# Four plain head jobs instead of eight, with the block sums formed in place

## The chip, the core and the metric

The kernel runs on one core of a Trainium2 chip, in one launch. The metric is device time in microseconds, median over runs; lower is better. The core has five engines with a queue each, which run side by side and wait for one another through semaphores: TensorE (PE, products, with its weight loads PEld), VectorE (DVE), ScalarE (ACT), GpSimd (POOL) and SyncE (SP, which here issues most DMAs).

## What is computed

One step of a hybrid decoder layer, in float32, for a prompt of 1024 tokens and for 8 samples of 4 tokens each. Cut to what matters:

```python
def layer(x, c, C0, n0, m0, k_past, v_past, ...):
    h, gate = adaln_in(x, c, w_ada, b_ada, g_norm)          # RMS norm, scale and shift from c
    (mq, mk, mv, mi, mf, mo, mz, aq, ak, av, az, gm, ga) = split_in(h @ w_in)
    y_m, C, n, m = mlstm_branch(mq, mk, mv, mi, mf, mo, mz, C0, n0, m0, ...)   # 4 heads, chunks of 128
    q, k = partial_rope(aq, pos), partial_rope(ak, pos)
    o = attn_prompt(q, k, v, sinks)                          # window of 128, 8 heads, 2 kv heads
    y_a = o * silu(az)
    u = sigmoid(gm) * (y_m @ w_mo) + sigmoid(ga) * (y_a @ w_ao)
    return x + gate * (u @ w_o), C, n, m, k_keep, v_keep     # then a final RMS norm
```

`h @ w_in` is the largest part. Its columns are cut into matrices of 128 columns: for each of the 4 mLSTM heads `mq`, `mk`, `mv`, `mo` and `mz`; `ak`, `av`, four `aq` and four `az` for the attention; eight `ga` and eight `gm` for the gates.

## The kernel before

**Exact products from two halves.** Each float32 operand is split into a high part and a low part of a faster format (`hi`, `lo`): ScalarE casts the high part, VectorE subtracts it for the low part. A product is then three matmuls: hi x hi, hi x lo, lo x hi.

**Plain jobs.** `job(n, ...)` multiplies the 128 columns of one matrix with all 1056 tokens: three pieces of 384, 384 and 288 columns (`PIECES`), in each 8 blocks of the depth with three matmuls, so 72 matmuls a job. While a job runs, the next one's weights are split (`prefetch`) and those of the one after are loaded (`preload`). `order` lists the plain jobs: `ak`, `av`, four `aq`, eight of the twelve head matrices, and later eight `w_mo`. The list `inner` has the head matrices in the order mq, mk, mv of head 0, then of head 1, and so on.

**Pairs of block products.** The other matrices go two by two through `block_products`: the 2 x 2 blocks of (depth half, token half) and the two matrices are multiplied in 7 block products in place of 8 (Winograd's form), each of 4 blocks of the depth with three matmuls of 512 columns. The products need sums of blocks of h: `t1` to `t4`, each with a high and a low part in half tiles. `sum_blocks` forms `t3`, `t2` and `t4` first, block by block of the depth (`k`), then `t1`, which takes the place of one block of h itself and must therefore wait until the last plain job is done. The samples' 32 columns go by themselves: 16 small products per pair (`Pair.samples`, tile `smp`) and one that gathers them (`samples_end`, tile `smpo`). Pairs in order: two of head matrices, eight `gate`, two `query_gate`, four `head_gate`.

**Half tiles.** `ht` hands out tiles of 128 x 512 from one pool of 43; x itself (16 tiles, `xT`), the sums, the attention's tiles and the heads' all come from it. After the setup x (by then h, scaled and shifted) is stored to `hD` in DRAM, and `sum_blocks` loads its blocks again from there.

**What fills the gaps.** The order of the instructions on each engine is written while the program is built. `Side` keeps a running clock `now`, an estimate that each matmul moves on, and a few streams of generators: "m" (gates, then the heads' recurrences `head(h)`, two at a time, 35 apart), "a" (the transposes of k and v, then 16 attention units `unit(g, b0)`, at most five at a time), "x" (`sum_blocks`, and `att_sums` at the end), "s" (the samples' attention, then the samples' heads `sample_head`), "g" (`ada_gate`, then `out_weights`). Between the matmuls of a job `side.tick()` takes a due generator one step on. Each `yield` names the time until the next step and the kind of PSUM bank that this needs. `side.finish` and `side.until` run a stream on where its result is needed. Loads and stores that SP issues stand in SP's one queue in the order in which they were written; most stores are put off by 8.0 (`store`).

**Where things stand.** `ada_gate` and `sample_attention` are added after the four query jobs; `sum_blocks` when the fourth job from the end of the plain ones begins (`i == -4`); the samples' heads when the last head is done (`h == NH-1`); the output weights at product 6 of pair 4 (`OUT_WEIGHTS`). With the last plain job (`i == -1`) the scores of the attention move from the bank kind "a" to "o", and the first pair is loaded.

## Time and profile before

| what | value |
|---|---|
| median of 3 runs | 844.07 us (842.58 to 844.69) |
| the profiled execution | 845.38 us, its span 843.6 us |
| PE busy | 823.8 us, 98% |
| DVE busy | 607.4 us, 72% |
| ACT busy | 417.2 us, 49% |
| POOL busy | 62.9 us, 7% |
| mean granted TensorE clock | 0.995 of full speed |
| DMA moved | 158.18 MB, mean 188 GB/s |

The span is the time between the first and the last instruction of the profiled execution; 1.8 us lie around it. Times of one instruction are given as the profile has them; successive instructions of an engine overlap a little, so a run of equal instructions, divided by their number, gives the price of one. Names such as `g_mk` or `bx` are the tiles that an instruction writes: `g_<matrix>` the result of a plain job, `bx`, `by`, `bw` and `bz` those of the block products, `sc`, `pt` and `oT` the attention's, `S`, `U`, `n` and `C` the heads'.

### The profile page before, as it was taken

The page shows a single profiled execution, that of the slowest core. Times are in us where ns is not written, and L with a number is a line of the kernel's source. Part 1 is how long each engine was busy: PE and PEld are TensorE (multiplying, and loading weights), DVE is VectorE, ACT ScalarE, POOL GpSimd, SP SyncE. Part 2 cuts the span into 40 slices and gives each one's busy share as a digit, 9 for nine tenths or more (in the row PEclk, how much of TensorE's full clock was granted, in tenths as well). Part 3 has the DMA queues.
Part 4 walks back from the last instruction along what each step waited for, and adds up shares of the span by engine and source line. Part 5 has one row for each costly group of instructions (what it writes and reads, how often), then busy time and mean ns, then how long its engine had stood idle before and what let it go on. Part 6 is the DMA issues. An engine that isn't in the chain of part 4 may idle for free.

```text
span 843.6 us, 15348 instructions
## 1 busy us (share of the span) xinstructions
PE 823.8 (98%) x5181; PEld 681.4 (81%) x5181; DVE 607.4 (72%) x1607; ACT 417.2 (49%) x1025; POOL 62.9 (7%) x108
## 2 busy tenths in 40 slices
PE   6999999999999999999999999999999999999996
PEld 2679989888899888888787777777777779997775
DVE  4786884655875775756676776788878998974676
ACT  4763356655664654545453534444436554334343
POOL 0120000001000000000000000000002104250000
PEclk9999999999999999999999999999999999999998
DMA  9996549257746553356456484555446676634522
GB/s 320 378 357 200 147 148 301 99 172 257 223 122 207 165 172 121 133 165 210 164 197 215 146 252 127 177 152 151 127 126 204 199 264 202 219 131 137 200 106 107
DMA packets 117859, 158.18 MB, mean 188 GB/s; under 512 B 29056, under 2 KB 64512, under 8 KB 117748
## 3 DMA queue, kind: packets, MB, share of 16 engines
q1 hardware_dynamic: 111556, 146.44, 54.1%
q10 hardware_dynamic: 4752, 6.56, 2.2%
q0 software_dynamic: 1472, 4.20, 1.3%
q8 instruction: 41, 0.67, 0.3%
q14 instruction: 38, 0.31, 0.1%
HBM read 113.41 MB, written 44.75 MB: 187 GB/s over the span
## 4 chain that ended last, share of the span: by engine, by line
PE 91%; DMA 4%; DVE 3%; ACT 1%; issue 1%; SPq 0%; DVEq 0%; ACTq 0%
PE by L258 10%; PE bx L258 10%; PE bw L258 9%; PE g_aq L258 6%; PE g_w_mo L258 6%; PE bz L258 5%; PE g_mq L258 4%; PE g_mk L258 4%; PE g_mv L258 3%; PE foW L258 3%; PE foX L258 3%; PE foY L258 2%; PE sc L258 2%; PE oT L258 2%; PE foZ L258 2%; PE smp L258 2%
## 5 line engine op out<-in xcount | busy, mean ns | idle before, releaser
L219 ACT ACTIVATE p<-p,nmx 128x256 f32<-128x256 f32 (+1 forms) x64 | 31.0, 486 | 23.9 <-DVE nmx L219 19.7
L258 PE MATMUL g_aq<-h_h,wh_aq 128*128 128x384 f32 (+1 forms) x96 | 32.4, 337 | 0.0
L219 DVE CUSTOM_DVE_ANT_0 p<-sc,cst,sink 128x256 f32<-128x256 f32 (+1 forms) x64 | 26.1, 463 | 7.4 <-PE sc L258 5.4
L258 PE MATMUL g_w_mo<-ym_l,wh_w_mo 128*128 128x384 f32 (+1 forms) x96 | 31.1, 324 | 0.0
L258 PE MATMUL g_aq<-h_l,wh_aq 128*128 128x384 f32 (+1 forms) x96 | 31.0, 323 | 0.0
L258 PE MATMUL g_w_mo<-ym_l,wl_w_mo 128*128 128x384 f32 (+1 forms) x96 | 31.0, 323 | 0.0
L258 PE MATMUL g_aq<-h_h,wl_aq 128*128 128x384 f32 (+1 forms) x96 | 31.0, 323 | 0.0
L258 PE MATMUL g_w_mo<-ym_h,wh_w_mo 128*128 128x384 f32 (+1 forms) x96 | 31.0, 323 | 0.0
L258 PE MATMUL g_mq<-h_h,wh_mq 128*128 128x384 f32 (+1 forms) x72 | 24.7, 343 | 0.0
L258 PE MATMUL g_mk<-h_h,wh_mk 128*128 128x384 f32 (+1 forms) x72 | 24.6, 342 | 0.0
L258 PE MATMUL g_mq<-h_l,wh_mq 128*128 128x384 f32 (+1 forms) x72 | 23.3, 323 | 0.0
L258 PE MATMUL g_mk<-h_h,wl_mk 128*128 128x384 f32 (+1 forms) x72 | 23.3, 323 | 0.0
L258 PE MATMUL g_mk<-h_l,wh_mk 128*128 128x384 f32 (+1 forms) x72 | 23.3, 323 | 0.0
L258 PE MATMUL g_mq<-h_h,wl_mq 128*128 128x384 f32 (+1 forms) x72 | 23.2, 322 | 0.0
L246 POOL DMA_DIRECT2D oD<-uqv x16 | 8.8, 551 | 147.1 <-ACT uqv L219 147.1
L258 PEld LDWEIGHTS g_aq<-h_h,wh_aq 128*128 128x128 f32 x96 | 18.0, 188 | 1.4 <-issue 1.2
L219 ACT ACTIVATE gt<-gt 128x512 f32<-128x512 f32 (+1 forms) x17 | 10.4, 612 | 16.9 <-DVE gt L219 16.2
L258 PEld LDWEIGHTS g_aq<-h_l,wh_aq 128*128 128x128 f32 x96 | 18.1, 188 | 0.0
L258 PEld LDWEIGHTS g_w_mo<-ym_l,wh_w_mo 128*128 128x128 f32 x96 | 18.0, 188 | 0.0
L258 PEld LDWEIGHTS g_w_mo<-ym_h,wh_w_mo 128*128 128x128 f32 x96 | 18.0, 188 | 0.0
L258 PEld LDWEIGHTS g_aq<-h_h,wl_aq 128*128 128x128 f32 x96 | 18.0, 188 | 0.0
L258 PEld LDWEIGHTS g_w_mo<-ym_l,wl_w_mo 128*128 128x128 f32 x96 | 18.0, 188 | 0.0
(1966 smaller groups left out, 2835.7 us busy)
## 6 DMA issues: line engine op xcount, KB each, us to landing
hb<-hD SPq DMA_DIRECT2D x24, 256.0 KB
x<-xT SPq DMA_DIRECT2D x16, 256.0 KB
early_h<-w_ada SPq DMA_DIRECT2D x8, 512.0 KB
adar_ga<-w_ada SPq DMA_DIRECT2D x16, 256.0 KB
wr_ga<-w SPq DMA_DIRECT2D x16, 256.0 KB
wr_gm<-w SPq DMA_DIRECT2D x16, 256.0 KB
taD<-gt SPq DMA_DIRECT2D x16, 256.0 KB
tmD<-gt SPq DMA_DIRECT2D x16, 256.0 KB
```

Source lines behind the costliest of these rows:

```text
L219: ins = f(*args, **kw)
L246: ins = (eng or nc.sync).dma_start(out, in_)
L258: in_order(nc.tensor.matmul(out, lhsT, rhs, start=start, stop=stop, skip_group_check=more))
```

## The change

Seven edits go together:

- Only the first four head matrices (`mq`, `mk`, `mv` of head 0 and `mq` of head 1) stay plain jobs; the other eight make four pairs.
- `sum_blocks` begins with the query jobs and no longer loads its blocks from `hD`: it forms the sums in the tiles of x. `t1` waits for a mark (`plain_ends`) that the last plain job sets when it begins; its blocks are still loaded.
- `ada_gate` begins with the query jobs too, and the samples' attention after them as before.
- The samples' heads are put in line when the second head is done, not the last.
- With the last plain job the attention's units are limited to three at a time.
- The output weights begin at pair 6 (of 18) instead of 4 (of 16): the same gate pair.
- Half tiles: 50 instead of 43, `C` tiles: 7 instead of 5; the room comes from GpSimd's descriptor space (`dynamic_dma_scratch_size=1024`).

```diff
--- before.py
+++ after.py
@@ -191,7 +191,7 @@
             return ps.tile(shape, F32, tag="o", bufs=2, name=name)
 
         def ht(shape, name, dt=F32):
-            return sp.tile(shape, dt, tag="half", bufs=43, name=name)
+            return sp.tile(shape, dt, tag="half", bufs=50, name=name)
 
         def sm(shape, name, bufs=3, dt=F32):
             return sp.tile(shape, dt, tag=name, bufs=bufs, name=name)
@@ -806,7 +806,7 @@
             dma(a["k_s"][124:128].rearrange("t b e -> b t e"), kns)
             dma(a["v_s"][124:128].rearrange("t b e -> b t e"), vns)
 
-        heads_done, samples_done, units_done, products_done = [], [], [], []
+        heads_done, samples_done, units_done, products_done, plain_ends = [], [], [], [], []
         oD = [dp.tile([128, SEQ], F32, name=f"oD{g}") for g in range(4)]
         osm = cp.tile([128, NH, NS], F32, name="osm")
         yaD = [dp.tile([128, T], F32, name=f"yaD{g}") for g in range(4)]
@@ -1006,11 +1006,11 @@
                 if (n, h) not in order:
                     return
                 i = order.index((n, h)) - order.index(None)
-                if i == -4:
-                    side.add("x", sum_blocks())
                 if i == -1:
+                    plain_ends.append(True)
                     side.finish("g")
                     sc_bank[:] = po, "o+"
+                    side.streams["a"]["max"] = 3
                     next(work)
                 job((n, h), keep(dst, smp, scale, "s"), (lambda: next(work)) if i == -1 else None)
                 head_part(h, 2)
@@ -1087,7 +1087,7 @@
                     mm(Un[:, i], kn[:, i * 128:i * 128 + 128], vn[:, i], start=True, stop=True)
                 chain = [C[0]]
                 for i, c in enumerate(cs):
-                    Cn = sm([128, 129], "C", 5)
+                    Cn = sm([128, 129], "C", 7)
                     if c:
                         V.scalar_tensor_tensor(Cn, chain[-1], dec[:, j0 + i:j0 + i + 1], Un[:, i], op0=ALU.mult, op1=ALU.add)
                     else:
@@ -1148,7 +1148,7 @@
             dma(a["C_p"][h], C[0][:, 0:128])
             dma(a["n_p"][:, h:h + 1], C[0][:, 128:129])
             heads_done.append(h)
-            if h == NH-1:
+            if h == 1:
                 for i in range(NH):
                     side.add("s", sample_head(i), "ob")
 
@@ -1296,24 +1296,21 @@
             names = "t3", "t2", "t4"
             for n in names:
                 blocks[n] = []
-            load = lambda k: block_load(((0, 0), (0, 1), (1, 0), (1, 1)), k)
-            nxt = load(0)
-            yield 7.0, ""
             for k in range(4):
-                b11, b12, b21, b22 = nxt
+                b11, b12, b21, b22 = (xT[th][4 * kh + k] for kh in range(2) for th in range(2))
                 for n in names:
                     block_tiles(n, k)
                 V.tensor_tensor(b22, b22, b12, op=ALU.subtract)
                 yield 2.5, ""
                 V.tensor_tensor(b11, b11, b22, op=ALU.add)
                 V.tensor_tensor(b21, b21, b11, op=ALU.subtract)
-                yield 5.0, ""
-                if k < 3:
-                    nxt = load(k + 1)
+                yield 4.0, ""
                 for n, t in zip(names, (b22, b11, b21)):
                     block_split(n, k, t)
-                    yield 2.5, ""
+                    yield 3.0, ""
             formed.append("t2")
+            while not plain_ends:
+                yield 0.5, ""
             load = lambda k: block_load(((0, 0), (0, 1)), k)
             ts = [load(0), load(1)]
             yield 3.0, ""
@@ -1558,8 +1555,8 @@
 
         order += [("ak", 0), ("av", 0)] + [("aq", g) for g in range(4)]
         inner = [(n, h) for h in range(NH) for n in ("mq", "mk", "mv")]
-        paired = list(zip(inner[8::2], inner[9::2]))
-        order += inner[:8]
+        paired = list(zip(inner[4::2], inner[5::2]))
+        order += inner[:4]
         order += [None] + [("w_mo", d) for d in range(KT)]
 
 
@@ -1977,15 +1974,16 @@
             if n == len(pairs) - 1:
                 next(att, None)
 
-        OUT_WEIGHTS = 4
+        OUT_WEIGHTS = 6
         LOADS = [(len(pairs) - 2, 7), (len(pairs) - 1, 5)]
         work = block_products(pairs, hook)
         att = att_products()
+        side.add("g", ada_gate())
+        side.add("x", sum_blocks())
+        blocks["t1"] = block(0, 1)
         for g in range(4):
             queries(g)
-        side.add("g", ada_gate())
         side.add("s", sample_attention(), "b")
-        blocks["t1"] = block(0, 1)
         for h in range(NH):
             head_jobs(h)
 
@@ -2298,7 +2296,7 @@
 
 
 def build(d):
-    nc = bacc.Bacc("TRN2", target_bir_lowering=False, num_devices=1)
+    nc = bacc.Bacc("TRN2", target_bir_lowering=False, num_devices=1, dynamic_dma_scratch_size=1024)
     aps = {}
     for k, v in d.items():
         aps[k] = nc.dram_tensor(k, v.shape, mybir.dt.from_np(v.dtype), kind="ExternalInput").ap()
```

## The prediction

> **What bounds the kernel now.** I read the page first: the busy shares, the clock digits and the chain that ended last.

> ```profile
> PE 823.8 (98%) x5181; PEld 681.4 (81%) x5181; DVE 607.4 (72%) x1607; ACT 417.2 (49%) x1025; POOL 62.9 (7%) x108
> PEclk9999999999999999999999999999999999999998
> PE 91%; DMA 4%; DVE 3%; ACT 1%; issue 1%; SPq 0%; DVEq 0%; ACTq 0%
> ```

> TensorE is busy for 98% of the span, at full clock, and carries 91% of the chain. So a change pays what it takes out of TensorE's queue, and costs whatever makes TensorE wait. VectorE comes next with 72%, but that is an average over stages, so I asked for windows: the tail of the setup (62 to 66), the four query jobs (66 to 120), the first head jobs (120 to 150), and two pairs of block products (279 to 325). The columns are the window, its length, then PE, PEld, DVE, ACT and POOL busy with counts, granted clock, DMA share and GB/s.

> ```profile
> 62.00:66.00 4.00, 4.00 (x47) 3.24 (x39) 1.82 (x6) 2.41 (x6) 0.00 (x0) 1.00 0.97 279
> 66.00:78.00 12.00, 11.99 (x79) 11.89 (x79) 8.96 (x35) 4.59 (x9) 0.20 (x1) 1.00 0.57 195
> 78.00:91.00 13.00, 13.00 (x84) 12.35 (x83) 9.61 (x35) 2.86 (x8) 0.00 (x0) 1.00 0.46 136
> 91.00:104.00 13.00, 13.00 (x83) 11.88 (x82) 10.15 (x34) 5.07 (x16) 0.00 (x0) 1.00 0.65 176
> 104.00:120.00 16.00, 16.00 (x110) 14.52 (x109) 13.97 (x58) 8.47 (x28) 0.71 (x1) 1.00 0.38 126
> 120.00:150.00 30.00, 30.00 (x229) 27.00 (x229) 16.64 (x69) 16.98 (x55) 1.39 (x3) 1.00 0.81 262
> 279.00:302.00 23.00, 22.37 (x146) 18.60 (x145) 20.17 (x64) 13.05 (x35) 0.92 (x3) 1.00 0.65 190
> 302.00:325.00 23.00, 23.00 (x144) 19.08 (x143) 15.53 (x48) 12.73 (x32) 1.18 (x3) 1.00 0.50 155
> ```

> TensorE has no idle time in any of them but the first pair. VectorE is busy 42.69 us of the 54 us of the query stage (79%), but only 16.64 of 30 in the head stage: the room for more VectorE work is in the head jobs, not in the query jobs.

> **TensorE's sum.** The chain in order of time gives the price of both kinds of job in pieces without interruption (start, us, what, instructions).

> ```profile
> 702.65 46.44 PE g_w_mo L258 x288
> 305.97 2.77 PE by L258 x12
> 319.72 1.01 PE smp L258 x32
> 316.72 0.17 PE smpo L258 x2
> ```

> *Removed.* A plain head job has 3 pieces of 24 products, two of 384 columns and one of 288. Four jobs fewer are 288 products, and the run of `w_mo` is just that: 288 products in the same two sizes, 46.44 us.

> *Added.* The four matrices go through two more pairs. A pair has 7 block products of 12 matmuls with 512 columns, 84 in all, so two pairs have 168 = 14 x 12, at 2.77 us per 12: 38.78 us. Each pair also brings the samples' sums by themselves, 1.01 us (16 small products; the row counts their weight loads too), and their gathering, 0.17 us: 2.36 us for two. That is 41.14 us.

> Net on TensorE: 46.44 - 41.14 = 5.30 us less. The instruction order of the changed kernel shows the same number of everything else on TensorE: scores, transposes, heads and samples' heads are moved, not dropped. The move takes the last six attention units and the heads into the pairs; interruptions are conserved, so I book nothing for them.

> **What is moved ahead onto VectorE and ScalarE.** The block sums (`sum_blocks`) now run during the query jobs, on the tiles of x themselves. In the changed order all 12 sums, 8 of the 12 low parts and 5 of the 10 row operations of `ada_gate` stand ahead of the first head job: 25 VectorE operations of 512 columns.

> ```profile
> 58.90 1.28 DVE L219 TENSOR_TENSOR wl_aq<-wr_aq,wh_aq 128x512 fp32r<-128x512 f32 x2
> 64.60 0.01 DVE L219 LOAD_MASK_SELECT ropet<-kr  x1 [2.15 <-ACT kr L219]
> 92.28 0.69 DVE L219 TENSOR_TENSOR wl_aq<-wr_aq,wh_aq 128x512 fp32r<-128x512 f32 x1 [0.34 <-ACT wh_aq L219]
> 105.49 0.34 PE L258 MATMUL g_aq<-h_h,wh_aq 128*128 128x384 f32 x1
> 100.60 0.55 DVE L219 TENSOR_SCALAR p<-p,den 128x128 f32<-128x128 f32 x2
> 110.11 0.27 PE L263 MATMUL pt<-cst,p 128*128 128x128 f32 x1
> ```

> Two such operations take 1.28 us, so 25 take 16.0 us. VectorE's idle time there is 11.31 us (54 - 42.69) and 2.18 us between 62 and 66, 13.49 us. So the stage is overfull by 2.5 us even if every gap can be filled. Who waits? The next job's weights: their low part ended at 92.97, and the job began at 105.49, 12.5 us of cover. The attention's transposes: the scaled scores were ready at 101.15, the transpose ran at 110.11, 9.0 us of cover. Being 2.5 us late is hidden. If no gap at all can be filled, VectorE is 16.0 us late, 9.0 of them covered, and TensorE loses 7.0 us. Between 0 and 7.0 I take 1.0 us: the gaps are real waits, like the 2.15 us for ScalarE's copy of `kr`, into which ready sums fit, and the head stage (13.36 us of idle VectorE in 30) takes up the arrears. If the cover of 9.0 us is gone, each further us costs one.

> The in-place sums also add waits. VectorE must not overwrite a tile of x before its store to `hD` has been read out, and behind that wait stand the last rotation of k and the next weights' low parts.

> ```profile
> 55.31 5.88 SPq L246 DMA_DIRECT2D hD<-x  x8
> 61.99 0.86 SPq L246 DMA_DIRECT2D kD<-krr  x1
> 66.31 0.20 POOL L219 MEMSET gt<- 32x128 f32 x1 [12.65 <-DMA kD<-krr]
> ```

> A store issued at 61.99 released its tile at 66.31, 4.3 us later. The first tile overwritten is the fifth of the eight stores, issued near 58.2, so free near 62.5 (estimate by the same 4.3 us); VectorE's own gap ran to 64.60. So at most 1 us of delay, inside the 1.0 booked. ScalarE's casts for the sums stand in a stage in which it is busy 21 of 54 us: nothing. `ada_gate` starts with the query jobs, and 14 of its 16 loads (256 KB each, 3.7 MB) are issued there: 13 us at the 279 GB/s of the first window, where the DMA engines are free for 27 of 54 us (one minus the DMA shares): nothing. The block `t1` is loaded at the start of the last plain job and first used by the seventh product of the first pair, over 12 us of plain job and six times 2.77 us later: nothing. More half tiles, two more `C` buffers and three attention units at a time in place of five only set when loads may start; I book nothing. The 16 loads from `hD` that vanish (256 KB each) were off the path: nothing. On SP's queue the loads of the pairs' weights stay ahead of their use by the same number of products.

> GpSimd's descriptor space is cut to 1,024 bytes. Of 16 writes of `oD` between 118.7 and 259.3 us one comes every 9 us and lands in 2.0 to 5.1 us, so no two are in flight: I take 0.

> ```profile
> L246 POOL DMA_DIRECT2D oD<-uqv x16: 539/539/710, 118.7 to 259.3; - x16
> DMA to landing us min/median/max: 2.0/3.6/5.1
> ```

> [...]

> **The stall that is already there.** The longest stretch of the chain off TensorE is in the gate pairs, where the output weights are prepared (`out_weights`).

> ```profile
> 400.14 3.15 DMA wor<-w_out
> 403.37 0.69 DVE wor L219
> 404.06 0.27 DVE C L219
> 404.38 1.12 PE S L258 x6
> 402.00:404.20 2.20, 0.41 (x4) 0.17 (x2) 0.94 (x3) 1.62 (x8) 0.10 (x1) 1.00 0.87 294
> 404.20:408.00 3.80, 3.62 (x13) 3.04 (x14) 2.92 (x14) 1.61 (x4) 0.00 (x0) 0.60 0.53 189
> 408.00:412.00 4.00, 4.00 (x22) 3.40 (x21) 3.47 (x16) 1.69 (x6) 0.00 (x0) 0.95 0.00 0
> ```

> VectorE waits in its queue for a weight's landing, the head's state update `C` stands behind it, and TensorE's `S` behind that. TensorE is idle 1.79 us, and then the granted clock is 0.60 for 3.80 us and 0.95 for 4.00, which loses 1.5 + 0.2 = 1.7 us. So such a stall costs 3.5 us, half of it afterwards. [...]

> The changed kernel starts `out_weights` in the same gate pair (pair 6 of 18 instead of 4 of 16), so I keep this stall as it is. But the samples' heads, now queued behind the second head, fall into the same pairs, with their loads on SP's queue and their operations on VectorE's.

> **The sum.** The profiled execution took 845.38 us (843.6 of span, 1.8 around it), 1.31 over the median of 844.07. 845.38 - 5.30 + 1.0 = 841.1; on the median's scale 839.8 us, 0.5% faster. What a measurement can tell here is 0.3%, 2.5 us: below 841.5 is faster, above 846.6 slower.

> **Rivals.**

> *VectorE becomes the bound of the query stage* (the slower side). It decides from the point where VectorE is over 9.0 us late at the scaled scores or 12.5 us at a weight. With no gap usable TensorE loses 7.0 us; in gaps like the one above, two of them drop the clock as well, 2 x 1.7: 10.4 in place of 1.0. 844.07 - 5.30 + 10.4 = 849.2 us. For it: 2.5 us overfull at best, and 12 sums come in one burst behind the waits for `hD`. Against it: the cover, and the half-empty head stage. Chance 0.15.

> *A second stall by the output weights.* The samples' heads add three state loads and three stores per head to the queue that was late at 400, and more VectorE work behind the same waits. One more stall of 3.5 us gives 839.8 + 3.5 = 843.3 us, no change. Against it: units and `hD` loads are no longer in the way of anything there. Chance 0.16.

> *The old stall goes away*, because head chain and output weights meet differently: 839.8 - 3.5 = 836.3 us. It needs only another order on VectorE at one place. Chance 0.13.

> *The change doesn't do what it says:* ruled out by the order, which has 288 plain products fewer and 168 block products more.

> **How the numbers follow.** The forecast, 837 to 841.5 us, has 0.56, the rivals 0.15, 0.16 and 0.13. Faster is forecast plus the vanished stall, 0.69; within 0.3% is the second stall, 0.16; slower is VectorE, 0.15. For 8 in 10 the range leaves out the slowest cases and a little at the bottom: from 835.0 (the stall gone and nothing lost early, 835.3) to 847.0 (the forecast with 7.0 us lost early and no clock drop is 845.8, and a little more).

> **What would show it.** Right: `g_mq`, `g_mk` and `g_mv` with 288 matmuls fewer; VectorE over 90% busy between 62 and 120 while TensorE stays without idle time; and the pairs starting at about 203 to 207 us, not 279, since the last four plain jobs began here:

> ```profile
> 202.37 3.17 PE g_mk L258 x18
> 279.16 2.78 PE bx L258 x12
> ```

>  Wrong: TensorE's idle time before `pt`, `oT` or `g_mq` ended by VectorE, a clock below 1.00 ahead of 150 us, or a second drop beside the one near 405. If plain and block products take other times than in the rows, the 5.30 is wrong, and with it everything.

## The result: 1.2% slower

The changed kernel takes 853.77 us (median of 5 runs, 850.41 to 856.03) against 843.85 us (842.58 to 844.69) for the kernel before: ratio 1.0116, 95% interval 1.0096 to 1.0136. I had forecast 839.8 us and a range up to 847.0. The time is outside the range, on the side to which I gave 0.15.

The page of the changed kernel, busy time and granted clock:

```profile
PE 823.4 (97%) x5129; PEld 668.2 (79%) x5129; DVE 613.6 (72%) x1629; ACT 421.9 (50%) x1032; POOL 60.9 (7%) x104
PEclk9999999999999999999999899999999999999998
```

TensorE has the 52 instructions fewer that the sum has (288 plain products gone; 168 block products, 64 `smp` and 4 `smpo` added), yet its busy time has hardly moved, 823.8 to 823.4 us: the digit 8 in the clock row is a slice at a lower clock, in which a block product of 512 columns starts 0.43 us behind the one before it in place of 0.23. That is 3.4 us (6.83 us at a granted clock of 0.50), against 1.7 before (3.41 us at 0.50), so only part of it. The span grew from 843.6 to 851.1 us.

The windows of the query stage, which answer to those of before, and the window that the forecast named:

```profile
66.00:78.00 12.00, 12.00 (x80) 11.94 (x79) 11.83 (x40) 4.79 (x10) 0.20 (x1) 1.00 0.78 270
78.00:91.00 13.00, 13.00 (x83) 12.36 (x83) 10.69 (x33) 3.71 (x9) 0.00 (x0) 1.00 0.60 191
91.00:104.00 13.00, 13.00 (x83) 9.87 (x83) 12.79 (x45) 5.82 (x20) 0.00 (x0) 1.00 0.70 172
104.00:122.90 18.90, 18.90 (x135) 17.50 (x135) 16.42 (x68) 11.22 (x36) 0.71 (x1) 1.00 0.58 182
62.00:120.00 58.00, 57.99 (x395) 52.37 (x395) 54.24 (x185) 24.92 (x70) 0.91 (x2) 1.00 0.69 210
```

VectorE is busy 51.73 of 56.90 us (91%), between 62 and 120 it is 54.24 of 58.00 (94%), and TensorE has no idle time. That part went as forecast.

Where the time went shows in a table by stage. For each kind and size of TensorE instruction I took the trimmed mean of the time from its start to the next start, over both traces; *work* is the number of instructions times that, *lost* is the length of the stage minus its work. Another trim moves a whole row by some us, but the differences between the columns only by some 1 us. The last two columns are two experiments told below (samples' heads behind the third head; and the output weights later as well). One run each of the experiments e1 and e2 took several times as long as the others (4555.70 and 2514.45 us); without it their medians are 861.75 and 845.56 us in place of the 862.65 and 845.62 given below.

| lost, us | before | after | e7 | e9 |
|---|---|---|---|---|
| query jobs | 2.5 | 3.1 | 3.1 | 3.1 |
| plain head jobs and head pairs | 12.9 | 17.8 | 18.0 | 17.9 |
| gate pairs | 10.8 | 19.7 | 11.1 | 7.9 |
| query-gate pairs | 1.5 | 3.5 | 1.7 | 1.7 |
| head-gate pairs and attention out | 5.3 | 4.3 | 4.9 | 5.5 |
| sum of lost | 33.1 | 48.4 | 38.8 | 36.0 |
| sum of work | 604.1 | 597.7 | 597.7 | 597.7 |

The change takes 6.4 us of work off TensorE and makes it lose 15.3 us more: 8.9 in the gate pairs, 4.9 ahead of them, 2.0 in the query-gate pairs. Up to the first gate pair it was 6.5 us ahead (317.50 against 323.97 us): 1.1 us of that it had before the query jobs began, and part it has because work stood later in the queue.

Names in the rows that follow: `gt` is the gate that a gate pair's product becomes; `wr_`, `wh_` and `wl_` are a weight as loaded and its high and low part, `wor` an output weight; `et`, `qw`, `hk` and `hv` are loaded for a head, `tk`, `tv`, `ty` and `yt` are further steps of it; `sz`, `qd`, `vf`, `vm`, `Cs`, `sn`, `sU` and `sty` belong to a sample head; `mx` belongs to the attention; `taD` is a gate in DRAM.

TensorE's waits (us in total, times, longest): the only two over 0.6 us behind the setup in the kernel before, then the three longest in the changed kernel.

```profile
PE S L258 <- DVE C L219: 2.0, 1, 2.0
PE bw L258 <- ACT bw L219: 0.9, 1, 0.9
...
PE bw L258 <- ACT bw L219: 4.1, 2, 3.1
PE smp L258 <- ACT yt L219: 2.7, 1, 2.7
PE pt L263 <- DVE mx L219: 1.5, 2, 1.0
```

**The stall at 404 us,** from the timeline: VectorE, ScalarE, TensorE, then a window over it.

```profile
399.90 0.56 DVE L219 TENSOR_TENSOR et<-et,cst 128x384 f32<-128x384 f32 x1 [0.81 <-DMA et<-nmd]
401.45 0.27 DVE L219 COPY sz<-stk 32x128 f32<-32x128 f32 x1
401.85 0.54 DVE L219 TENSOR_TENSOR vf<-sz,wm 32x387 f32<-32x387 f32 x1
404.11 0.42 DVE L219 TENSOR_TENSOR vf<-sz,wm 32x258 f32<-32x258 f32 x1
405.39 0.29 DVE L219 CAST vm<-vf 32x258 fp32r<-32x258 f32 x1
405.71 0.69 DVE L219 TENSOR_TENSOR gt<-p,bw 128x512 f32<-128x512 f32 x1
...
404.91 0.61 ACT L219 CAST wh_pgate__5005<-wr_ga 128x512 fp32r<-128x512 f32 x1
406.48 0.63 ACT L219 ACTIVATE gt<-gt 128x512 f32<-128x512 f32 x1 [0.96 <-ACT wh_pgate__5005 L219]
407.02 0.58 ACT L219 COPY bw<-bx 128x512 f32<-128x512 f32 x1
407.65 0.50 PE L258 MATMUL bw<-t2h,wh_pgate__4874 128*128 128x512 f32 x1 [3.15 <-ACT bw L219]
404.00:407.60 3.60, 0.51 (x4) 0.25 (x2) 3.43 (x9) 2.15 (x5) 0.00 (x0) 1.00 0.15 40
```

Read it from the bottom. TensorE waits 3.15 us for ScalarE's copy `bw`. ScalarE has it behind `gt<-gt`, which needs VectorE's `gt<-p,bw`. (The profile puts ScalarE's wait down to the cast before it; that cast had ended at 405.52, the `gt` of VectorE ended at 406.40.) VectorE runs without a gap of 0.1 us from 399.90 to 406.40: a head's `et` and `qw`, a weight's low part, two `C`, and between 401.45 and 405.68 the first visit of a sample head, eleven of its thirteen instructions, 3.8 us. The `gt` that empties the gate pair's bank stands behind all of it.

**The stall at 470 us:** a product and VectorE ahead of it, SyncE's longest waits between 462 and 466 us, its queue, then VectorE, ScalarE, TensorE and a window behind it.

```profile
455.93 0.39 PE L258 MATMUL bw<-h_h,wl_pgate__5456 128*128 128x512 f32 x1
456.81 0.27 DVE L219 COPY sz<-stk 32x128 f32<-32x128 f32 x1
461.18 0.69 DVE L219 TENSOR_TENSOR gt<-p,bw 128x512 f32<-128x512 f32 x1
...
SPq L246 <- ACT gt L219: 5.1, 1, 5.1
SPq L246 <- DVE wr_ga L219: 1.9, 1, 1.9
...
462.61 0.32 SPq L246 DMA_DIRECT2D taD<-gt  x1
464.84 0.33 SPq L246 DMA_DIRECT2D wr_ga<-w  x1
466.69 0.38 SPq L246 DMA_DIRECT2D et<-nmd  x1
471.43 0.42 DVE L219 TENSOR_TENSOR et<-et,cst 128x256 f32<-128x256 f32 x1 [1.52 <-DMA et<-nmd]
471.88 0.69 ACT L219 ACTIVATE et<-et,an 128x128 f32<-128x128 f32 x2 [6.20 <-DVE et L219]
472.63 0.58 ACT L219 ACTIVATE yt<-ty,vec 128x384 f32<-128x384 f32 x1
473.26 0.30 PE L258 MATMUL smp<-wr_ga,c 128*32 128x128 f32 x2 [2.70 <-ACT yt L219]
474.40:481.30 6.90, 6.42 (x15) 5.00 (x16) 4.16 (x9) 1.21 (x4) 0.00 (x0) 0.51 0.70 205
```

The same in-order queues, with a transfer in front. SyncE first stands 5.1 us for a gate result of ScalarE that it is to store (`taD<-gt`), then 1.9 us for VectorE's `wr_ga`, the last use of a tile into which the next weight is to be loaded. That gate result was late for the reason seen at 404: the product `bw` ended at 456.32, but VectorE's `gt<-p,bw` began at 461.18, behind another sample head's first visit that had begun at 456.81; ScalarE could finish the gate only then. The head's loads stand behind both waits, `et` lands late, ScalarE stands still for 6.20 us, TensorE for 2.70, and then it runs at half clock for 6.8 us, which loses 3.4 more. The two stalls cost 3.15 + 2.70 + 3.4 = 9.3 us; the one of before cost 3.5. These 5.8 us more are two thirds of the 8.9 us that the gate pairs lose more; TensorE's other waits there are 0.9 us in all for `tv` and less for each of the rest, and what else is lost was not followed.

### The profile page after: what moved, and what is told of

Same layout as the page of the kernel before. It is cut to its first block, busy times and chain, and to the rows that moved or that the text cites. A ratio compares the mean times of both kernels' runs of the same rounds, so it can differ in the third digit from the quotient of the medians.

```text
span 851.1 us, 15206 instructions
## 1 busy us (share of the span) xinstructions
PE 823.4 (97%) x5129; PEld 668.2 (79%) x5129; DVE 613.6 (72%) x1629; ACT 421.9 (50%) x1032; POOL 60.9 (7%) x104
## 4 chain that ended last, share of the span: by engine, by line
PE 49%; issue 3%; DVE 2%; DMA 2%; ACT 1%; SPq 1%; POOL 0%; ACTq 0%; DVEq 0%; POOLq 0%
PE by L258 8%; PE bx L258 7%; PE bw L258 7%; PE g_w_mo L258 5%; PE bz L258 4%; PE foW L258 3%; PE foX L258 3%; PE foY L258 2%; PE foZ L258 2%; PE ay L258 1%; PE aw L258 1%; PE ax L258 1%; PE smp L258 1%; PE n L258 1%; SPq L246 1%
## 5 line engine op out<-in xcount | busy, mean ns | idle before, releaser
L219 ACT ACTIVATE p<-p,nmx 128x256 f32<-128x256 f32 (+1 forms) x64 | 31.0, 485 | 16.6 <-DVE nmx L219 16.4
L258 PE MATMUL g_aq<-h_h,wh_aq 128*128 128x384 f32 (+1 forms) x96 | 32.4, 338 | 0.0
L258 PE MATMUL g_w_mo<-ym_l,wh_w_mo 128*128 128x384 f32 (+1 forms) x96 | 31.1, 324 | 0.0
L258 PE MATMUL g_aq<-h_l,wh_aq 128*128 128x384 f32 (+1 forms) x96 | 31.0, 323 | 0.0
L258 PE MATMUL g_w_mo<-ym_l,wl_w_mo 128*128 128x384 f32 (+1 forms) x96 | 31.0, 323 | 0.0
L258 PE MATMUL g_aq<-h_h,wl_aq 128*128 128x384 f32 (+1 forms) x96 | 31.0, 323 | 0.0
L258 PE MATMUL g_w_mo<-ym_h,wh_w_mo 128*128 128x384 f32 (+1 forms) x96 | 31.0, 323 | 0.0
L219 DVE CUSTOM_DVE_ANT_0 p<-sc,cst,sink 128x256 f32<-128x256 f32 (+1 forms) x64 | 26.1, 463 | 4.2 <-PE sc L258 4.1
L219 ACT ACTIVATE et<-et,an 128x128 f32<-128x128 f32 x32 | 11.1, 394 | 23.6 <-DVE et L219 23.3
L246 POOL DMA_DIRECT2D oD<-uqv x16 | 9.0, 560 | 183.6 <-ACT uqv L219 183.6
L219 DVE COPY p<-pt 128x512 f32<-128x512 f32 (+1 forms) x16 | 10.5, 655 | 15.1 <-PE pt L263 15.1
L258 PEld LDWEIGHTS g_aq<-h_h,wh_aq 128*128 128x128 f32 x96 | 18.0, 188 | 2.6 <-issue 1.5
L219 DVE TENSOR_TENSOR wor<-wor,gb 128x512 f32<-128x512 f32 x16 | 11.0, 688 | 10.3 <-DMA wor<-w_out 10.3
L219 ACT ACTIVATE p<-p,den 128x256 f32<-128x256 f32 (+1 forms) x32 | 14.4, 489 | 7.3 <-DVE den L219 7.1
L258 PEld LDWEIGHTS g_aq<-h_l,wh_aq 128*128 128x128 f32 x96 | 18.1, 188 | 0.0
L258 PEld LDWEIGHTS g_w_mo<-ym_l,wh_w_mo 128*128 128x128 f32 x96 | 18.0, 188 | 0.0
L258 PEld LDWEIGHTS g_w_mo<-ym_h,wh_w_mo 128*128 128x128 f32 x96 | 18.0, 188 | 0.0
L258 PE MATMUL sc<-ukv,uqv 64*128 64x256 f32 (+1 forms) x128 | 18.0, 390 | 0.0
L258 PEld LDWEIGHTS g_aq<-h_h,wl_aq 128*128 128x128 f32 x96 | 18.0, 188 | 0.0
L258 PEld LDWEIGHTS g_w_mo<-ym_l,wl_w_mo 128*128 128x128 f32 x96 | 18.0, 188 | 0.0
L263 PE MATMUL pt<-cst,p 128*128 128x128 f32 x120 | 16.5, 277 | 1.5 <-DVE mx L219 1.5
L258 PE MATMUL g_mq<-h_h,wh_mq 128*128 128x384 f32 (+1 forms) x48 | 16.8, 351 | 0.3 <-ACT mk L219 0.3
```

Source lines behind the costliest of these rows:

```text
L219: ins = f(*args, **kw)
L246: ins = (eng or nc.sync).dma_start(out, in_)
L258: in_order(nc.tensor.matmul(out, lhsT, rhs, start=start, stop=stop, skip_group_check=more))
L263: in_order(nc.tensor.transpose(out, in_, idn))
```

## Experiments

All times are medians beside runs of the kernel before on the same chip (843.2 to 843.9 us), so a difference between two experiments on different chips is known to some 0.8 us. Edits are against the changed kernel unless said otherwise.

**e1, e7: the place of the samples' heads.**

```diff
-            if h == 1:
+            if h == NH-1:      # e1; in e7: if h == 2
```

> The changed kernel with one part undone: the samples' heads are put in line behind the last head again, not behind the second. Theory: the samples' heads beside heads 2 and 3 and the output weights make the two stalls of TensorE at 404 and 470 us (3.15 us; 2.70 us and then 6.8 us at half clock, so 3.4 us more); without them some 9 us go and the time is 843 to 846 us. Rival, that the four plain jobs fewer crowd the pairs whatever stands in line: 851 to 855 us, with the stalls in other places.

e1: 862.65 us, 1.0225 [1.0208, 1.0242]. The stall at 470 is gone and the one at 404 is 0.6 us, but the time is worse. TensorE's waits of e1:

```profile
PE sty L263 <- DVE sns L219: 17.7, 2, 15.4
```

Each head-gate pair needs one more sample head done; four of them in a row behind the last head end so late that the last pair waits 15.4 us. So my undoing added a cost of its own, and neither theory had that. Reckoned as in the table, e1 loses some 12 us less than the change in the gate pairs and some 22 us more in the head-gate pairs. With 18 pairs the samples' heads must stand earlier than that.

> The changed kernel with the samples' heads put in line behind the third head, between the change's place and the old one. By the order they end in the second query gate's or the first head gates' pairs. Theory that only their overlap with the output weights and heads 2 and 3 costs: 843 to 847 us. Rival that they must be early, since the last pairs wait for them: over 850 us, with a wait for sty in the head gates' pairs as when they stood behind the last head (17.7 us there).

e7: 842.81 us, 0.9984 [0.9966, 1.0001], 11.0 us less than the change, at a mean granted clock of 0.997 to 0.999 (the change: 0.989 to 0.994). So 11.0 us hang on the place of the samples' heads alone, and a place between the two is better than both.

**e3, e4: the parts in the kernel before.** e4 has the 50 half tiles and the descriptor space of 1,024 bytes alone; e3 also 7 `C` tiles and `if h == 1`.

> The kernel before with the memory edits alone: 50 half tiles and the descriptor space of 1,024 bytes. Theory: no cost, 842 to 845 us. Rival, that the smaller descriptor space or the longer turn of the half tiles slows loads: 848 us or more.

e4: 843.23 us, 0.9997 [0.9988, 1.0007]. The memory edits cost nothing.

> The kernel before (eight plain jobs) with the samples' heads put behind the second head, and with the 50 half tiles, the smaller descriptor space and the 7 C buffers of the change, which it needs for that. Theory that the place of the samples' heads makes the stalls: 849 to 855 us, with late et loads and a second clock drop. Rival that the fewer plain jobs do: 842 to 845 us.

e3: 849.49 us, 1.0069 [1.0050, 1.0089]. Its waits of TensorE:

```profile
PE sU L258 <- DVE Cs L219: 4.2, 1, 4.2
PE bw L258 <- ACT bw L219: 2.0, 1, 2.0
```

With eight plain jobs the early samples' heads cost 6.3 us (849.49 against e4), at a mean granted clock of 0.991 to 0.996 (e4: 0.995 to 0.999). The stalls lie in other places, but the fewer plain jobs are not needed for the damage.

**e2, e9: the output weights' place.** e2 starts them in the eleventh pair; e9 does that with e7's place of the samples' heads.

```diff
-        OUT_WEIGHTS = 6
+        OUT_WEIGHTS = 10
```

> The changed kernel with the output weights' stream put into the eleventh pair instead of the seventh, the samples' heads left where the change puts them. If the stalls need the output weights beside the samples' heads: 844 to 848 us, no stall of over 2 us before 430 us. If heads and samples' heads alone make them: 850 to 855 us, with both stalls still there.

e2: 845.62 us, 1.0030 [1.0016, 1.0044]. Both stalls are gone; a new one came, in which `by` waits 3.0 us from 548 us on, behind a sample head's first visit on VectorE.

> The changed kernel with the samples' heads behind the third head and the output weights in the eleventh pair: the fourth corner beside 853.8 us (neither moved), 845.6 us (weights moved) and 842.8 us (samples' heads moved). If the two moves take away the same stall: 841 to 844 us, little beyond 842.8. If each took away its own: 835 us.

e9: 841.37 us, 0.9972 [0.9960, 0.9984].

| | weights in 7th pair | in 11th pair |
|---|---|---|
| samples' heads behind 2nd head | 853.8 (the change) | 845.6 (e2) |
| behind 3rd head | 842.8 (e7) | 841.4 (e9) |

Either move takes most of it away, 11.0 or 8.2 us, and both together 12.4: it is the meeting that costs. Windows of the change, then the same of e9:

```profile
395.00:410.00 15.00, 11.85 (x59) 9.33 (x61) 12.45 (x29) 6.73 (x14) 0.00 (x0) 1.00 0.71 214
440.00:481.00 41.00, 37.76 (x245) 29.69 (x244) 32.23 (x94) 17.82 (x49) 1.72 (x7) 0.92 0.61 194
```

```profile
395.00:410.00 15.00, 14.35 (x74) 11.80 (x73) 7.70 (x15) 8.60 (x21) 0.65 (x2) 1.00 0.50 170
440.00:481.00 41.00, 41.00 (x245) 33.38 (x246) 29.34 (x89) 21.08 (x52) 2.17 (x8) 1.00 0.43 127
```

In the first window VectorE falls from 83% to 51% busy and TensorE gets 2.5 us back.

**Transfers or VectorE's instructions?** Five runs.

```diff
-                yield 6.0, ""       # out_weights, from loads to multiplications
+                yield 14.0, ""      # e6
-                    V.tensor_tensor(t, t, gb[f], op=ALU.mult)
+                    (left out)      # wa
-                        dma(raws[k, f], a["w_out"][k * 128:(k + 1) * 128, HALF[f]])    # left out in wb
-                    V.tensor_tensor(t, t, gb[f], op=ALU.mult)
+                    V.tensor_tensor(t, gb[f], gb[f], op=ALU.mult)       # wb
```

> The changed kernel with the 24 multiplications of the output weights by the gate left out (so the output is not the reference's), their loads, sums and stores kept. If VectorE's instructions of that stream make the stalls near 404 and 470 us: 844 to 848 us, as when the stream was moved (845.6). If its transfers in SyncE's queue make them: 851 to 855 us.

wa: 843.84 us, 1.0016 [0.9997, 1.0035], with a mean granted clock of 0.998 in the profiled execution (the change: 0.993). (The trace of the change has 16 such multiplications; the 24 counts in the 8 sums, which stayed.) Of the two stalls 0.6 us near 405 and 0.5 us near 467 are left; in total, TensorE's waits for `bw` are:

```profile
PE bw L258 <- ACT bw L219: 1.5, 2, 0.9
```

> The changed kernel with the 16 loads of the output weights left out (the multiplications run on a tile that is there, so the output is not the reference's), all VectorE instructions and stores kept. If the transfers and VectorE's waits for them make the stalls: 844 to 848 us. If VectorE's instructions do: 851 to 855 us, with VectorE's 10.3 us of waits for wor gone all the same.

wb: 848.83 us, 1.0069 [1.0045, 1.0093]. Leaving out the loads gives back 4.9 us, half of the 9.9 that wa gives back. TensorE's waits of wb:

```profile
PE bw L258 <- ACT bw L219: 3.9, 2, 3.0
```

The first stall stays (3.0 us), the one at 470 is gone. So taking VectorE's multiplications (and with them its waits for `wor`) out is enough; taking the transfers out is not. The transfers alone cost nothing that can be seen (wa), the multiplications alone about half (wb), and the other half needs both.

e5 keeps everything and spreads the sample head's first visit:

```diff
-                V.tensor_copy(vm[64:96, :w], vf[:, :w])
-                vms.append((vf, vm, w))
-            yield 3.0, ""
-            ...             # et; the casts and the subtractions, each in a loop of its own
+                S.copy(vm[0:32, :w], vf[:, :w])
+                vms.append((vf, vm, w))
+                ...         # et, in the first group
+                yield 2.5, ""
+                V.tensor_copy(vm[64:96, :w], vf[:, :w])
+                V.tensor_tensor(vm[32:64, :w], vf[:, :w], vm[0:32, :w].bitcast(F32), op=ALU.subtract)
+                yield 1.5, ""
```

> The changed kernel with a sample head's first visit cut into four: its three groups of value tiles (three VectorE instructions and a ScalarE cast each) are issued 4 us apart and not in one burst; nothing is left out. Theory that bursts in VectorE's in-order queue make the stalls (sample head, output weights and head stages issued at one time): 846 to 850 us, the 3.15 us stall near 404 us gone. Rival that late transfers through SyncE's one queue make them: 852 to 856 us, with VectorE's waits for et and wor by DMA as before (9.0 and 10.3 us).

e5: 847.77 us, 1.0052 [1.0036, 1.0069]: 6.0 us back, though VectorE still waits 7.8 us for `et` and 7.8 for `wor` by DMA. TensorE's waits of e5:

```profile
PE tk L263 <- ACT yt L219: 3.1, 1, 3.1
PE bw L258 <- ACT bw L219: 2.9, 2, 2.0
```

The stall near 404 is 2.0 us instead of 3.15 and the one at 470 is gone, but the next `tk`, 0.6 us in the change, waits 3.1 at 412: less, not gone as I expected.

> The changed kernel with the output weights' multiplications issued 14 us behind their loads instead of 6 us, so that VectorE finds them landed; the same transfers and the same instructions. Theory of late transfers (VectorE stands still for wor, ScalarE and TensorE behind it): 844 to 849 us, VectorE's wait for wor under 2 us. Rival that the number of VectorE instructions in these pairs makes the stalls: 851 to 855 us with wor's wait gone all the same.

e6: 850.31 us, 1.0077 [1.0052, 1.0102]. This one missed both ranges: VectorE's waits for `wor` stayed at 9.5 us and those for `et` rose to 13.7. The edit put the multiplications later, not the loads earlier, and it did not take the wait away that it was to take away. It tells the theories apart only weakly.

e14ab moves `(load, 1)` and `(load, 2)` one visit ahead.

> The changed kernel with the loads of each head's second and third group issued one visit earlier (7 and 5 us more lead), all else as the change has it. Theory of late transfers: VectorE's 9.0 us of waits for et go under 3 us and the time is 845 to 849 us. Theory that VectorE's and ScalarE's instructions of three streams at one place are enough: 850 to 855 us though the waits for et are shorter.

e14ab: 869.24 us, 1.0311 [1.0284, 1.0338]; neither theory had that. VectorE's and TensorE's waits:

```profile
DVE et L219 <- DMA et<-nmd: 22.5, 9, 4.4
...
PE bw L258 <- ACT bw L219: 14.2, 3, 9.4
```

The waits for `et` rose from 9.0 to 22.5 us, so the edit did not do what it was for. But its longest stall is the purest of all: TensorE is idle 9.4 us from 410.2, while VectorE runs (first and last row of 23) without waiting for any transfer:

```profile
408.76 0.56 DVE L219 TENSOR_TENSOR qw<-qw,hq 128x384 f32<-128x384 f32 x1
...
417.65 0.67 DVE L219 TENSOR_TENSOR gt<-p,bw 128x512 f32<-128x512 f32 x1
```

The sample head's first visit, three `C`, weights' low parts and sums, and again `gt` last.

**Two more on what is left.** e8 has `OUT_WEIGHTS = 10` and e5's spreading; sp12 the same with 12; e11b is e8 with four attention units at once instead of three.

> The changed kernel with the output weights put into the eleventh pair and the samples' heads' first visit cut into four as well. With the output weights moved alone it was 845.6 us with one stall of 3.0 us at 548 us behind a burst of a sample head on VectorE. If bursts are the cause that stall goes: 840 to 843 us, the forecast of the sum. Otherwise 845 to 847 us.

> The kernel of 841.5 us with the output weights in the thirteenth pair instead of the eleventh, so that they begin some 45 us later, behind the last head's stages. If any overlap of the three streams still costs there: 839 to 841 us. If nothing is left of it: 841 to 843 us; if the weights now meet the last loads of the pairs: over 844 us.

> The kernel of 841.5 us (output weights in the eleventh pair, the samples' first visit cut) with four attention units at once in the pairs instead of three. The stretch from the plain head jobs to the first gate pair loses 17.8 us to interruptions after the change and 12.9 us before it. If the limit of three causes that: 836 to 839 us, with under 15 us lost there. If it is the mixing of attention with pairs itself: 840 to 843 us.

e8: 841.47 us, 0.9972 [0.9957, 0.9986]; the 3.0 us stall of e2 is gone. sp12: 841.90 us, 0.9980 [0.9966, 0.9995], no different. e11b: 844.76 us, 1.0018 [0.9995, 1.0041], 3.3 us more than e8 and outside both ranges; it loses as much ahead of the gate pairs as the change does, within 0.5 us, so the limit of three is not the reason for that loss. e8 and e9 beat both kernels, the one before by 0.28%.

## Why the prediction was wrong

**TensorE's sum was right.** 5.30 us less was forecast; the table has 6.4 us less work, which by the choice of the trim is known to some 1 us. One row I had misread: the 32 `smp` are 32 matmuls, two for each of the 16 small products, and their weight loads are counted apart as PEld. The price of the row, 1.01 us, is the same.

**The query stage was right.** I booked 1.0 us, bounds 0 to 7.0; it lost 0.6 us more than before with VectorE at 91%, and the pairs began at 205.5 us (203 to 207 forecast). The rival on the slower side had the right direction for a reason that the runs don't bear out: it is VectorE that TensorE waits for, but in another stage.

**What was booked at nothing** for the half tiles and the descriptor space was nothing (e4). "Interruptions are conserved, so I book nothing for them" was a second step that failed, by 4.9 us ahead of the gate pairs. TensorE's idle time there grew by 1.7 us (2.8 against 1.1), with `pt` waiting for VectorE's `mx` (1.5 us) and `bw` (0.9); the rest is in the spacing of `pt` and the block products. e7 and e9 lose the same there. Its cause stays open, except that the limit of three units is not it (e11b).

**The step that failed** is "I keep this stall as it is", with the price of the rival *a second stall by the output weights*. The mechanism was named there, samples' heads and output weights in the same queues. But I took it for one more stall of 3.5 us with chance 0.16, and argued that "units and `hD` loads are no longer in the way". Moving the samples' heads alone is worth 11.0 us (change against e7). I had seen that they "fall into the same pairs" and did not count VectorE there, as I had done for the query stage. The trace of before holds what was needed: VectorE was at 20.17 of 23.00 us in the first pair, and a sample head's first visit could have been added up from its own rows further down, 4.7 us of VectorE from 518.51 on. In the query stage such lateness was covered by 9 to 12 us; here `gt`, `bw` and the next product had too little cover, and TensorE waited 3.15 us. What the runs show in place of one stall of 3.5 us: the meeting of the samples' heads with the output weights costs 8.2 to 12.4 us, in bursts on VectorE and in the lateness that they pass on to SyncE's queue.

**Two signs that I had named against me** came, in other places. The second clock drop was not beside the old one: at 404 there was none this time, at 474 there was one twice as long (6.83 us against 3.41). And TensorE was idle before `pt`, 1.0 us near 246 and 0.5 us near 289, ended by VectorE's `mx`: in the pairs, not in the query stage that the sign was meant for.

**e9 gives the forecast a second reading.** With both moves the time is 841.4 us, 1.6 above the forecast: the sum was that of a kernel in which these streams do not meet. That it comes so near is in part luck, for two errors offset each other: by the table e9 loses 5.0 us more ahead of the gate pairs than the kernel before, which I had booked at nothing, and 2.9 us less in them, where I had kept the old stall.

## What to carry to other kernels

When a change moves a stream of work, make the busy time of the slower engines by stage for its new place, not only for the stage that you worry about. The instructions that free TensorE's bank here (`gt` and `bw`) ran only when everything issued ahead of them on VectorE and ScalarE had run: at 404 us `gt` stood behind 5.8 us of VectorE's work (399.90 to 405.71), and TensorE waited 3.15 us. So spread bursts (e5 gave 6.0 us back), and keep two bursts out of one pair (e9 gave 12.4). Try the place of a stream before judging the change that moved it: the same edits are 1.2% slower or 0.3% faster.

## What the runs showed of the hardware

```profile
402.76:406.18 3.42, 1.75 (x10) 1.20 (x8) 3.25 (x9) 2.27 (x5) 0.00 (x0) 1.00 0.36 122
406.18:409.59 3.41, 1.94 (x9) 1.61 (x9) 3.35 (x8) 1.72 (x3) 0.00 (x0) 1.00 0.35 107
409.59:413.00 3.41, 3.41 (x30) 2.35 (x29) 0.48 (x2) 1.01 (x3) 0.00 (x0) 1.00 0.55 184
471.03:474.44 3.41, 1.11 (x33) 0.85 (x33) 2.52 (x8) 2.56 (x8) 0.54 (x1) 1.00 0.62 220
474.44:477.85 3.41, 2.94 (x7) 2.17 (x8) 3.41 (x8) 1.07 (x3) 0.00 (x0) 0.50 0.46 145
```

The 3.15 us wait is split into 1.67 and 1.47 us of idle time in two windows, and the clock stays; the shorter one lies nearly whole in one window, with 2.30 us idle, and the next is at half clock. Between 60 and 835 us of the traces of both kernels two windows had more than 1.67 us idle: the one with 2.30 us, and one with 1.97 us in the kernel before (401.58 to 404.99). Both were followed by a granted clock of 0.50, and no window at full clock with 1.67 us or less was. In e5 windows with 2.04 and 2.94 us idle, and in e14ab one with 2.79 us, were followed by 0.50 too. So here the cost of a stall depended on where it fell in these windows, by an estimate from these rows 1.7 us for one window at half clock. Executions of one kernel differ in their clock: the kernel before had a mean of 0.995 in its profile with the drop near 405, and of 0.995 to 0.999 in its 25 runs beside those of e9. Whether it is this drop that comes and goes there, no trace shows. Why the drop at 474 lasts two windows is open, since the first of them has only 0.47 us idle.
